# Output projection of a decoder trunk in seven block products, with channels instead of tokens on the partitions

## The chip, the cores and the metric

The kernel runs on one core of a Trainium2 chip. The metric is the time of one execution in device microseconds. The core has a tensor engine (PE, with its weight loads as PEld), a vector engine (DVE), a scalar engine (ACT), GpSimd (POOL) and a queue for transfers (SP). Each works through its own queue in order and waits on semaphores. All data are fp32. A product in full precision is made of three fp32r products of high and low parts: x = xh + xl, w = wh + wl, and x w is taken as xh wh + xl wh + xh wl. The high part is a copy rounded to fp32r, the low part the difference. So each operand of a product costs a copy (ACT) and a subtraction (DVE) before PE can use it, or a copy, an accumulating DMA issued by POOL, and another copy (`split_dma`).

## The reference

Sequence and model width are 1024, the MLP's width is 4096.

```python
        h = rms_norm(x, g_mix[l])
        z = jnp.einsum("bsd,de->bse", h, w_in[l]) + b_in[l]
        ...
        y_a = jnp.einsum("bsc,cd->bsd", u, w_a_out[l])
        ...
        y_b = jnp.einsum("bsc,cd->bsd", v * jax.nn.gelu(gb), w_b_out[l])
        m = jax.nn.sigmoid(sa) * y_a + jax.nn.sigmoid(sb) * y_b
        x = x + jnp.einsum("bsd,de->bse", m, w_o[l])
        h = rms_norm(x, g_mlp[l])
        f = jnp.square(jax.nn.relu(jnp.einsum("bsd,df->bsf", h, w_1[l])))
        x = x + jnp.einsum("bsf,fd->bsd", f, w_2[l])
    return rms_norm(x, g_final)
```

The change lies between `m` and the first products of `w_1`.

## The kernel before

Tokens are split into even and odd ones (two halves of 512), channels into two halves of 512. The products with `w_a_out`, `w_1` and `w_2`, and part of those with `w_in`, are done in a form with seven block products instead of eight: a 2 x 2 block matrix product in which sums and differences of blocks are formed first on either side. A block product here is twelve matmuls (four slices of 128 channels, three products of parts each) of 128 x 128 by 128 x 512, into one PSUM bank. Sums that several outputs share are carried on by copying a bank into another and accumulating further.

The product with `w_a_out` (names beginning with `g_`, lines 1112 to 1239) runs 7 x 4 such blocks: for each of the seven products in the order `GORD`, four pairs of 128-row output tiles. The loop at the end of this part takes a block n a step: it handles what block n-1 left (`g_post`: bank copies on ACT, outputs on DVE), issues block n (`g_mm`), makes the weight parts of block n+4 (`g_lhs`) and the weight sums of block n+5 (`g_sums`), then what the table `GX` lists for this step (`g_parts`: high and low part of a right-hand block; `g_t`: a sum of right-hand blocks; loads). DVE's work goes through `later` and is put out at the step's end by `vector_work`, sorted by the time at which it is expected to be ready. This stage is scheduled by hand (`tc.manual_schedule`): each engine's queue has the order of the text. Its result, multiplied by the gate and added to the other branch, is `m`, channels on partitions.

The output projection with `w_o` is done with tokens on partitions, and in eight blocks: `o_first` takes four token tiles at once through the eight channel slices while `w_o` is loaded and split (`load_wo`), `o_proj` the other four one after the other; 384 matmuls. `residual` adds a row tile of x, takes the sum of squares along the row on ACT, the inverse root (`rms_rows`), scales the row tile, and stores it for the end of the kernel (`x1d`, by a DMA of POOL). Then `transposed` turns the scaled rows by PE into channel tiles, 64 transposes, and `h2_block` evicts them with the gain. The first half's transposes stand between two tiles of the output projection, the second half's after the first two up blocks.

The up products (`up_step`, `up_mm`, `up_lhs`) run for 16 pairs of tiles, seven blocks each; for the first four pairs products 1 and 2 of all come first (they need only the even tokens), then the other five. The down projection follows.

SBUF tiles of 4 KB a partition come from a pool of 37 (`T`) and one of 12 (`M`), half tiles from one of 14 (`EV`); PSUM has eight banks.

## Time and profile before

| | |
|---|---|
| time, median of 3 runs | 1577.55 us (1577.54 to 1577.6) |
| the profiled execution's own time | 1577.67 us |
| its span, first to last instruction | 1575.9 us |
| PE busy | 1552.0 us (98%), 6862 matmuls |
| PEld busy | 1274.2 us (81%) |
| DVE busy | 1179.8 us (75%), 1611 instructions |
| ACT busy | 868.4 us (55%) |
| POOL busy | 156.9 us (10%) |

Busy times are of one profiled execution; matmuls overlap, so PE's busy time is not the time at its peak. The columns of the chain of waits are start, length, engine, tile, line and count; those of the list of waits are the waiting instruction, what it waited for, the total, the count and the longest; those of a timeline are start, length, engine, line, operation, output and input, shape and count, in brackets the idle time before and what ended it; those of a window are its length, then for each engine its busy time and instructions (PE, PEld, DVE, ACT, POOL), the granted clock, the DMA engines' busy share and GB/s. A row of the transfers gives issuing queue, count, size and median time from issue to landing.

### The profile page before, as it was taken

How to read it: one execution, taken by the hardware profiler on the slowest of the kernel's cores; microseconds unless marked ns; L12 is line 12 of the kernel's file. 1: busy time of each engine (PE TensorE's matmuls, PEld its weight loads, DVE VectorE, ACT ScalarE, POOL GpSimd, SP SyncE). 2: the span in 40 equal slices, each digit the busy share in tenths (PEclk: the TensorE clock that was granted, in tenths of full speed). 3: DMA queues.
4: the chain of work that ended last, by engine and by line, in shares of the span. 5: the costliest groups of instructions: out<-in, count | busy, mean ns of one | idle time of the engine just before them, and what ended most of it. 6: DMA issues, size and time to landing. Idle time of an engine off the chain costs nothing.

```text
span 1575.9 us, 19026 instructions
## 1 busy us (share of the span) xinstructions
PE 1552.0 (98%) x6862; PEld 1274.2 (81%) x6862; DVE 1179.8 (75%) x1611; ACT 868.4 (55%) x1183; POOL 156.9 (10%) x190
## 2 busy tenths in 40 slices
PE   8999999999999999999999999999999999999997
PEld 6888778788888888878888877888888888888886
DVE  6799999979899997378667247855554458888897
ACT  5547575667567667345376146554444475555552
POOL 0000000002222222000031000000000001111110
PEclk9999999999999999999999999999999999999999
DMA  9667868899998779944578532533334669888852
GB/s 368 166 158 182 228 178 220 207 266 245 242 249 202 192 187 257 310 148 133 193 184 228 183 112 77 213 113 115 107 108 134 192 215 230 217 223 226 205 121 107
DMA packets 119855, 301.00 MB, mean 191 GB/s; under 512 B 12064, under 2 KB 29984, under 8 KB 119760
## 3 DMA queue, kind: packets, MB, share of 16 engines
q1 hardware_dynamic: 93488, 226.92, 43.9%
q0 software_dynamic: 26128, 72.59, 23.9%
q8 instruction: 54, 0.88, 0.2%
q14 instruction: 41, 0.34, 0.1%
q10 hardware_dynamic: 144, 0.26, 0.1%
HBM read 148.21 MB, written 58.72 MB: 131 GB/s over the span
## 4 chain that ended last, share of the span: by engine, by line
PE 88%; DVE 4%; ACT 3%; issue 2%; DMA 2%; SPq 0%; POOL 0%; ACTq 0%; POOLq 0%; DVEq 0%
PE d L1736 15%; PE z L678 11%; PE yb L1032 8%; PE o L1337 3%; PE e L1851 2%; PE keep L1736 2%; PE o L91 2%; PE z L258 2%; DVE v L438 1%; PE o L1361 1%; PE rg L486 1%; PE rg L488 1%; PE rg L487 1%; DVE y L589 1%; DMA g<-g 1%
## 5 line engine op out<-in xcount | busy, mean ns | idle before, releaser
L678 PE MATMUL z<-xh,win_h 128*128 128x512 f32 x400 | 123.4, 390 | 0.0
L678 PE MATMUL z<-xl,win_h 128*128 128x512 f32 x400 | 123.2, 389 | 0.0
L1748 DVE TENSOR_TENSOR acc<-acc,d 128x1024 f32<-128x1024 f32 x72 | 87.9, 1220 | 33.4 <-PE d L1736 32.7
L678 PE MATMUL z<-xh,win_l 128*128 128x512 f32 x400 | 98.1, 391 | 0.0
L589 DVE SCALAR_TENSOR_TENSOR y<-u,vec,y 128x511 f32<-128x511 f32 (+14 forms) x120 | 88.8, 740 | 0.0
L678 PEld LDWEIGHTS z<-xh,win_l 128*128 128x128 f32 x400 | 75.1, 188 | 16.9
L678 PEld LDWEIGHTS z<-xh,win_h 128*128 128x128 f32 x400 | 75.1, 188 | 16.2
L678 PEld LDWEIGHTS z<-xl,win_h 128*128 128x128 f32 x400 | 75.1, 188 | 15.8
L589 DVE SCALAR_TENSOR_TENSOR yt<-u,vec,yt 128x511 f32<-128x511 f32 (+6 forms) x112 | 82.9, 740 | 0.0
L589 DVE SCALAR_TENSOR_TENSOR y<-yt,csum,y 128x511 f32<-128x511 f32 (+6 forms) x112 | 82.9, 740 | 0.0
L494 ACT ACTIVATE g<-rg,vec 96x1024 f32<-96x1024 f32 x32 | 35.6, 1113 | 84.8 <-PE rg L488 44.5
L1529 ACT ACTIVATE fa<-fa 128x512 f32<-128x512 f32 x16 | 10.1, 632 | 89.8 <-DVE fa L1507 89.8
L438 DVE SCALAR_TENSOR_TENSOR v<-xb,vec,v 128x1023 f32<-128x1023 f32 (+2 forms) x36 | 46.2, 1283 | 16.5 <-ACT v L429 15.7
L1469 ACT ACTIVATE o<-s 128x512 fp32r<-128x512 f32 x64 | 38.2, 624 | 29.4 <-DVE s L1461 26.1
L66 POOL DMA_DIRECT2D win_l<-win_raw x25 | 21.8, 872 | 316.2 <-ACT win_l L65 238.2
L1032 PE MATMUL yb<-hgh,wb_h 128*128 128x512 f32 x168 | 52.5, 394 | 0.0
L1032 PE MATMUL yb<-hgl,wb_h 128*128 128x512 f32 x168 | 51.7, 389 | 0.0
L66 POOL DMA_DIRECT2D zo<-zw x42 | 36.8, 879 | 129.0 <-ACT zo L65 115.8
L998 DVE TENSOR_TENSOR o<-w_raw,o 128x512 fp32r<-128x512 f32 x40 | 27.5, 690 | 29.2 <-ACT o L1469 29.2
L998 DVE TENSOR_TENSOR o<-s,o 128x512 fp32r<-128x512 f32 x64 | 42.6, 687 | 4.7 <-ACT o L1469 4.6
L1372 DVE TENSOR_TENSOR x<-xr,o 128x1024 f32<-128x1024 f32 x8 | 9.7, 1219 | 44.6 <-PE o L1337 30.2
L1032 PE MATMUL yb<-hgh,wb_l 128*128 128x512 f32 x168 | 41.0, 389 | 0.0
(1629 smaller groups left out, 4572.7 us busy)
## 6 DMA issues: line engine op xcount, KB each, us to landing
fr<-fd SPq DMA_DIRECT2D x32, 512.0 KB, 5.9
wr<-in_w_dram SPq DMA_DIRECT2D x32, 512.0 KB, 6.4
w_raw<-in_w_dram SPq DMA_DIRECT2D x31, 512.0 KB, 4.4
zw<-in_w_in_dram SPq DMA_DIRECT2D x28, 512.0 KB, 6.9
win_raw<-in_w_in_dram SPq DMA_DIRECT2D x25, 512.0 KB, 6.8
win_l<-win_raw POOLq DMA_DIRECT2D x25, 512.0 KB, 5.8
zo<-zw POOLq DMA_DIRECT2D x42, 256.0 KB, 5.6
gates<-zg SPq DMA_DIRECT2D x32, 256.0 KB, 4.2
```

Of the source, the lines that this page charges most:

```text
L66: nc.gpsimd.dma_start(l, src, accum_op=ALU.add)
L91: nc.tensor.matmul(ps[:, HALVES[hf]], a, b[hf], start=i == 0, stop=i == len(todo) - 1)
L438: nc.vector.scalar_tensor_tensor(v[:, d:S], a[:, 0:S - d], cbw_c[:, w * 12 + t:w * 12 + t + 1], v[:, d:S], ALU.mult, ALU.add)
L494: nc.scalar.activation(a, gps.pop((n, gi))[:HD, :], AF.Sigmoid, bias=(ba_c, bx_c)[gi][:, n:n + 1])
L589: nc.vector.scalar_tensor_tensor(o[:, k:], a[:, 0:HS - k], c, o[:, k:], ALU.mult, add)
L678: nc.tensor.matmul(zps[s][:, HALVES[hf]], w[:, k, :], xw[k][part][hf], start=n == 0, stop=n == 23)
L998: tt(l, src, h.bitcast(F32), ALU.subtract)
L1032: nc.tensor.matmul(ps[hf], a, b[:, HALVES[hf]], start=n == 0, stop=n == len(todo) - 1)
L1337: nc.tensor.matmul(ps[:, HALVES[hf]], tok(a, k, t), wo[k][b][:, HALVES[hf]], start=k == 0 and b == 0 and n == 0, stop=k == 7 and b == 1)
L1469: nc.scalar.activation(o[:, 0], src, AF.Copy)
L1736: nc.tensor.matmul(o, a, b, start=n == 0 and (p != 1 or g == 0), stop=n == len(todo) - 1, skip_group_check=p == 1 and g > 0)
L1748: tt(acc[p, q2], acc[p, q2], ps, ALU.add)
```

## The change

The output projection becomes a second pass of the seven-product form: all `g_` functions take a letter, "a" for `w_a_out` on the conv branch, "o" for `w_o` on `m`, "u" for the first two products of four pairs of up tiles. One list of 28 + 28 + 8 blocks runs through the same loop. `m` is loaded in the half-token layout (16 transfers of 256 KB instead of 8 of 512 KB), the order of the seven products becomes 1, 2, 6, 7, 4, 5, 3. The output `x1` has channels on partitions; x is loaded transposed (`xt_eo`, a new input) and added to. The rms is taken from channel tiles: ACT squares each output (`x1_squares`), DVE adds the squares of eight tiles, PE sums over partitions with a column of ones (`x1_sums`), a root on 128 x 4 (`x1_root`), and PE spreads its diagonal over the partitions (`x1_spread`); `x1_normed` scales each tile on DVE. The row tiles that the end of the kernel needs are made by 64 transposes of `x1` beside blocks u0 to u5 (`x1_rows`), evicted by ACT and stored by SP. The blocks for products 6, 5, 7, 3, 4 of the first two pairs of up tiles are interleaved; their weight parts, and those of product 2 in the new loop, are made by `split_dma` instead of DVE. `o_first`, `o_proj`, `residual`, `rms_rows`, `transposed`, `h2_block`, `h2_sum`, `h2_parts` and `first_lhs` go away. PSUM banks stay one pool to the end of the up products.

The core of the diff:

```diff
-    GORD = (1, 2, 6, 5, 3, 7, 4)
+    GORD = (1, 2, 6, 7, 4, 5, 3)
...
+    gseq = [(w, i, p) for w in "ao" for p in GORD for i in range(GP)]
+    gseq += [("u", i, p) for p in (1, 2) for i in range(AHEAD)]
...
+        if p in (1, 7) or w != "u" and p == 2:
             nc.scalar.activation(o[:, 0], src, AF.Copy)
             later(at("A", 0.6), 0.63, low, o[:, 1], src, o[:, 0])
         else:
             split_dma(src, o[:, 0], o[:, 1])
...
         else:
+            d = x1[i // 2, o, i % 2][:, HALVES[m_]]
+            later(0, 0.63, tt, d, d, src, ALU.add)
+            squares.append((o, d))
...
     def g_post(w, i, p):
...
+            gb[*k, "f"], gb[*k, "u"] = bank(f"g{w}{i}f"), EV(f"gu{w}{i}")
+            nc.scalar.activation(gb[*k, "f"], gb[*k, "b"], AF.Copy)
+            nc.scalar.activation(gb[*k, "u"], gb[*k, "b"], AF.Copy)
             at("A", 1.24)
+        elif p == 7:
+            gb[*k, "c"] = EV(f"gc{w}{i}")
+            nc.scalar.activation(gb[*k, "c"], gb[*k, "f"], AF.Copy)
+            at("A", 0.62)
+        elif p == 4:
+            g_out(w, i, 1, 0, gb[*k, "f"])
+        else:
+            c = gb[*k, "c" if p == 5 else "u"]
+            later(0, 0.63, tt, c, c, gb[*k, "e"], ALU.add)
+            g_out(w, i, int(p == 5), 1, c)
...
+    def x1_squares():
+        while squares:
+            o, d = squares.pop(0)
+            tile_ = EV if o == 0 else lambda n: T(n)[:, 0:HS]
+            sqn[0] += 1
+            a = tile_(f"xs{o}_{sqn[0]}")
+            nc.scalar.activation(a, d, AF.Square)
+            ready = at("A", 0.62)
+            if o not in ss:
+                ss[o] = a
+            else:
+                later(ready, 0.63, tt, ss[o], ss[o], a, ALU.add)
+    def x1_sums(o):
+        rbk[o] = bank(f"ss{o}")
+        for i in range(4):
+            nc.tensor.matmul(rbk[o][:, i:i + 1], ss[o][:, i * P:(i + 1) * P], ones[:, 0:1],
+                             start=True, stop=True)
+        at("P", 0.5)
+    def x1_root(o):
+        st = cp.tile([P, 4, 4], F32, tag="st4", name=f"stm{o}", bufs=2)
+        v, s, t, r = (st[:, i, :] for i in range(4))
+        nc.vector.tensor_scalar(v, rbk[o][:, 0:4], 1.0 / D, EPS, ALU.mult, ALU.add)
+        newton_rstd(r, v, s, t)
+        at("V", 1.5)
+        ss[o] = rd = EV(f"rdm{o}") if o == 0 else T(f"rdm{o}")[:, 0:HS]
+        for i in range(4):
+            d = rd[:, i * P:(i + 1) * P]
+            if i % 2 == 0:
+                nc.vector.tensor_scalar(d, ident, r[:, i:i + 1], None, ALU.mult)
+            else:
+                nc.scalar.activation(d, ident, AF.Copy, scale=r[:, i:i + 1])
+        at("V", 0.4)
+    def x1_spread(o):
+        rbk[o] = bank(f"rbm{o}")
+        for i in range(4):
+            d = slice(i * P, (i + 1) * P)
+            nc.tensor.matmul(rbk[o][:, d], ones, ss[o][:, d], start=True, stop=True)
...
+    def x1_normed(kk, o):
+        for c2 in range(2):
+            src = x1[kk, o, c2]
+            hq[kk, o, c2] = a = src if o else T(f"hq{kk}{o}{c2}")
+            for i in range(2):
+                c = 4 * kk + 2 * c2 + i
+                dve(0.68, 0, nc.vector.scalar_tensor_tensor, a[:, HALVES[i]], src[:, HALVES[i]],
+                    gmlp_c[:, c:c + 1], rbk[o], ALU.mult, ALU.mult)
+    def x1_rows(t):
+        rows, c0 = T(f"x1r{t}"), t % 4 * P
+        for kk in range(2):
+            ps = bank(f"tr{t}{kk}")
+            for c in range(4):
+                nc.tensor.transpose(ps[:, c * P:(c + 1) * P],
+                                    x1[kk, t // 4, c // 2][:, c % 2 * HS + c0:c % 2 * HS + c0 + P],
+                                    ident)
+            nc.scalar.activation(rows[:, HALVES[kk]], ps, AF.Copy)
+            at("A", 0.62)
+        nc.sync.dma_start(x1d[t], rows)
...
     def up_lhs(i, p):
...
+        if i < 2:
+            split_dma(src, o[:, 0], o[:, 1])
+        else:
+            nc.scalar.activation(o[:, 0], src, AF.Copy)
+            low(o[:, 1], src, o[:, 0])
...
+          13: ((m_load, 0, 1),), 14: ((g_parts, "a", 5, 0), (m_load, 1, 1)),
+          15: ((g_parts, "a", 5, 1),), 18: ((g_parts, "a", 3, 0), (g_load, "o", 0, 0)),
+          19: ((g_parts, "a", 3, 1), (g_load, "o", 1, 0)), 20: ((g_load, "o", 2, 0),),
+          21: ((g_load, "o", 3, 0), (g_parts, "o", 1, 0)), 22: ((g_parts, "o", 1, 1),),
+          23: ((g_load, "o", 0, 1),), 24: ((g_parts, "o", 2, 0), (g_load, "o", 1, 1)),
+          25: ((g_parts, "o", 2, 1), (g_load, "o", 2, 1)), 26: ((g_load, "o", 3, 1),)}
+    o0 = GP * 7
+    GX.update({o0 + n: v for n, v in {
+        1: ((g_t, "o", 0, 1),), 2: ((g_t, "o", 0, 2), (g_t, "o", 1, 1), (x_in, 0, 0)),
+        3: ((g_t, "o", 1, 2), (x_in, 1, 0)), 4: ((g_parts, "o", 6, 0),), 5: ((g_parts, "o", 6, 1), (g_t, "o", 0, 3)),
+        6: ((g_t, "o", 1, 3),), 8: ((g_parts, "o", 7, 0), (g_t, "o", 0, 4)),
+        9: ((g_parts, "o", 7, 1), (g_t, "o", 1, 4)), 12: ((g_parts, "o", 4, 0),),
+        13: ((g_parts, "o", 4, 1), (x_in, 0, 1)), 14: ((x_in, 1, 1),), 16: ((g_parts, "o", 5, 0),),
+        17: ((g_parts, "o", 5, 1), (up_load, 0, (0,))), 18: ((up_load, 1, (0,)),),
+        19: ((g_parts, "o", 3, 0), (up_load, 2, (0,))), 20: ((g_parts, "o", 3, 1), (up_load, 3, (0,))), 22: ((x1_sums, 0),), 23: ((x1_root, 0),),
+        24: ((x1_spread, 0),), 25: ((x1_normed, 0, 0),), 26: ((g_parts, "u", 1, 0), (g_parts, "u", 1, 1),
+                                                             (x1_normed, 1, 0)),
+        27: ((g_parts, "u", 2, 0), (g_parts, "u", 2, 1))}.items()})
+    u0 = 2 * o0
+    GX.update({u0 + n: v for n, v in {
+        0: ((x1_rows, 4), (x1_sums, 1), (x1_rows, 5), (x1_root, 1)),
+        1: ((x1_rows, 6), (x1_rows, 7), (x1_spread, 1), (x1_normed, 0, 1)),
+        2: ((x1_rows, 0), (x1_normed, 1, 1), (g_t, "u", 0, 1), (g_t, "u", 1, 1)),
+        3: ((x1_rows, 1), (g_t, "u", 0, 2), (g_t, "u", 1, 2), (up_load, 0, (1,))),
+        4: ((x1_rows, 2), (g_parts, "u", 6, 0), (up_load, 1, (1,))), 5: ((x1_rows, 3), (g_parts, "u", 6, 1)),
+        6: ((g_parts, "u", 5, 0), (up_lhs, 0, 6)), 7: ((g_parts, "u", 5, 1), (up_lhs, 1, 6))}.items()})
...
+            x1_squares()
             g_get(n - 1, g_post)
+            if n == u0:
+                vector_work(clk["V"])
+                to_mlp()
...
+    useq = [(i, p) for p in ORDER[1:4] + (3, 4) for i in range(2)]
+    useq += [(i, p) for i in range(2, AHEAD) for p in ORDER[1:4] + (3, 4)]
+    useq += [(i, p) for i in range(AHEAD, NP) for p in ORDER]
+    UX = {0: ((g_t, "u", 0, 3), (g_t, "u", 1, 3)), 1: ((g_parts, "u", 7, 0), (g_parts, "u", 7, 1)),
+          2: ((g_t, "u", 0, 4), (g_t, "u", 1, 4)), 3: ((g_parts, "u", 3, 0), (g_parts, "u", 3, 1)),
+          5: ((g_parts, "u", 4, 0), (g_parts, "u", 4, 1))}
```

525 lines of the change are left out of this document (184 added, 341 removed).

## The prediction

> **What bounds the kernel now.** I read the page first, then the chain of work that ended last, the tensor engine's waits, and the vector engine's timeline.
>
> ```profile
> span 1575.9 us, 19026 instructions
> PE 1552.0 (98%) x6862; PEld 1274.2 (81%) x6862; DVE 1179.8 (75%) x1611; ACT 868.4 (55%) x1183; POOL 156.9 (10%) x190
> 774.17 2.72 PE g0a L1171 x12
> ...
> 850.96 43.52 PE o L1337 x192
> 894.48 22.03 PE o L91 x96
> ...
> 943.75 3.01 PE f0a L1478 x12
> 949.49 3.49 PE tr_m L1407 x32
> ...
> 1256.09 5.44 PE keep L1736 x24
> ```
>
> TensorE (PE) is the bound: 98% busy, and the chain lies on it. 192 products take 43.52 us, 0.2267 us each; I call twelve of them (2.72) a block. A transpose costs 3.49/32 = 0.109. The change works between 774.17, where the product with w_a_out starts, and 1256.09, where the down projection starts. From 850.96 PE has 384 products of the output projection (`o`), 1344 up products and 64 transposes: 87.0 + 304.6 + 7.0 = 398.7 us, in 405.1. So 6.5 us are lost there, 4.1 of it in these waits (without g3e's, which lies before 850.96) and the rest in slow restarts and late operands (f0a's twelve take 3.01 instead of 2.72: 0.3 for a restart):
>
> ```profile
> PE f0a L1478 <- DVE x L1372: 1.4, 1, 1.4
> PE f0c L1478 <- DVE fa L1505: 1.0, 1, 1.0
> PE f0c L1478 <- DMA b3l<-hq: 0.8, 1, 0.8
> PE f0d L1478 <- DVE fa L1507: 0.6, 1, 0.6
> PE g3e L1171 <- DMA ga<-gs: 0.3, 1, 0.3
> PE o L91 <- ACT hq L1401: 0.3, 1, 0.3
> ```
>
> **What PE gains.** The seven-product form needs 4 x 7 blocks = 336 products instead of 384. The 64 transposes stay (now they make the residual's rows). Added are 16 small products for the sums of squares (two instructions for each fp32 product) and 16 for spreading the root:
>
> ```profile
> 6.86 0.56 PE L312 MATMUL spare<-stx,ones 128*128 128x1 f32 x2 [6.86 <-ACT x L201]
> 7.28 5.04 PE L316 MATMUL spare<-ident,ones 128*128 128x128 f32 x22
> 14.31 1.50 PE L316 MATMUL spare<-ident,ones 128*128 128x128 f32 x12
> 32.33 1.06 PE L224 MATMUL rb<-rd,ones 128*128 128x128 f32 x8
> ```
>
> Eight of L224's take 0.9 from start to start, so 1.8 for the spread of both halves. The sums' products have one column instead of 128; the only such row is L312's (two in 0.56, with PE just woken), so a half's eight cost between 0.9 and 2.2; I take 0.9, since here PE comes straight from other products: 1.8 again. Without any wait the end of the up products is at 774.17 + 672 x 0.2267 (152.3) + 304.6 + 7.0 + 3.6 = 1241.7: 14.4 us earlier. The question is how much of it VectorE (DVE) and the transfers take back.
>
> **What DVE must do for it.** Its real price is the distance from start to start:
>
> ```profile
> 781.87 0.69 DVE L414 TENSOR_TENSOR gs<-wa,wa 128x512 f32<-128x512 f32 x1
> 782.60 0.69 DVE L414 TENSOR_TENSOR gs<-gs,wa 128x512 f32<-128x512 f32 x1
> 783.33 0.69 DVE L414 TENSOR_TENSOR wa<-wa,gs 128x512 f32<-128x512 f32 x1
> 783.94 0.68 DVE L414 TENSOR_TENSOR wa<-wa 128x512 f32<-128x512 f32 x1
> 784.54 1.22 DVE L414 TENSOR_TENSOR q<-q,q 128x1024 f32<-128x1024 f32 x1
> 785.67 0.69 DVE L998 TENSOR_TENSOR ga<-wa,ga 128x512 fp32r<-128x512 f32 x1
> 35.48 0.74 DVE L228 SCALAR_TENSOR_TENSOR xc<-xc,vec,rb 128x512 f32<-128x512 f32 x1
> 36.14 0.69 DVE L233 TENSOR_TENSOR xl<-xc,xh 128x512 fp32r<-128x512 f32 x1
> ```
>
> 512 columns: 0.61, or 0.72 when the next needs its result; 1024 columns: 1.13; scaling by the root: 0.66. The rows above stand in the order of the text, each as soon as the one before lets it, so the queue can be walked by adding. I number blocks a0-a27 (w_a_out), o0-o27, u0-u7 (first up products), and add up the queue block by block against 2.72.
>
> First pile, a21 to o9. From a21 to a27 the outputs, the high/low parts of m and of w_o come to 21.3 in 19.0: 2.3 behind at o0. o0 to o9 come to 2.7, 1.7, 2.9, 4.4, 3.8, 5.5, 4.4, 1.2, 4.1, 3.5 = 34.2: o3, for one, has a pair's four weight sums (2.7), one sum of m (1.1) and a low part (0.6); o5 an output (0.6), four weight sums, a sum of m and product 6's second low part (1.1 each). So the last of them, the low part of product 7's second half, is done 36.5 after the start of o0. o12 starts at 12 x 2.72 = 32.6 and needs it with its eighth product, at about 34.3: PE waits 2.2. (With 2 us more or less in the pile it would be 0 to 4.) After that DVE has slack to o20.
>
> Second pile, counted from the start of o20. PE does o20-o22 and the sums of squares (8.2 + 0.9 = 9.1). The root (`x1_root`) stands in DVE's queue ahead of the outputs of o22 and all that follows, so DVE, done with o21's outputs at 6.8, idles until then, and everything behind waits with it. What the root costs:
>
> ```profile
> 28.14 0.17 DVE L208 TENSOR_SCALAR stx<-stx 128x4 f32<-128x4 f32 x1 [1.39 <-ACT x L201]
> ...
> 29.59 0.48 DVE L215 TENSOR_SCALAR rd<-ident,stx 128x128 f32<-128x128 f32 x2
> 710.68 1.28 ACT L96 ACT_TABLE_LOAD   x1 [6.75 <-DVE lv L1095]
> ```
>
> 1.9 from 28.14 to 30.07, and 1.3 for the table of the square root, which started only when its operand was there: DVE is free at 12.4. The outputs of products 5 and 3 then cost 1.33 a block, squares 0.61, the low part of an up weight 0.61; beside them stand eight scalings (5.3) and four low parts (4.5) of the normed block. Queue: outputs and squares of o22 (1.9) and o23 with a low part (2.6) to 16.9, at o25 four scalings and the like to 22.1 (5.2), o26 to 27.3 before its two low parts, which end at 28.4 and 29.5, o27 to 34.3, last output 35.7, last sum of squares 36.9. PE, after o24, the spread and three blocks, wants the first low part at 23.7: it waits 4.7. u0 ends at 28.4 + 11 x 0.2267 = 30.9. Next in PE's queue stand eight transposes of a row tile of the second half, the last four of which need the output done at 35.7, and the second half's sums of squares, due 31.8, started 36.9: 5.1 more, and u1 stands behind it. From there PE's own work (sums, 8 x 8 transposes, spread, u1-u7) covers the second half's root and scalings, and ends 63.9.
>
> Up weights of the first two pairs go through GpSimd's (POOL's) accumulating DMA instead of DVE:
>
> ```profile
> ga<-gs POOLq DMA_DIRECT2D x8, 256.0 KB, 3.3
> ga<-wa POOLq DMA_DIRECT2D x8, 256.0 KB, 7.2
> 785.59 0.62 ACT L65 ACTIVATE ga<-gs 128x512 fp32r<-128x512 f32 x1
> 786.11 0.63 ACT L67 ACTIVATE ga<-gs 128x512 fp32r<-128x512 f32 x1
> 788.78 1.05 ACT L1123 ACTIVATE g5h<-q 128x1024 fp32r<-128x1024 f32 x1
> 812.00:832.00 20.00, 19.68 (x88) 15.94 (x87) 12.62 (x17) 13.43 (x23) 5.26 (x6) 1.00 1.05 266
> 774.00:851.00 77.00, 76.68 (x338) 63.17 (x337) 59.43 (x81) 48.38 (x79) 16.63 (x19) 1.00 0.84 220
> ```
>
> Block (0,6)'s sums stand behind product 6's second low part, whose high part ScalarE (ACT) makes only after it has evicted the last row tile (59): high part 60, low 61.1, sums 62.5, copy 63.1, landing 3.3 later 66.4; PE wants it at 64.3. With the next block 2.6 in all. 3.3 is the row of the same kind of source; with 7.2 it would be 6.5.
>
> Free by their cover: ACT (48.4 of 77 us busy in the first product, the fourth pair of the window's row) takes the 16 squares, 0.52 each. x comes in as 8 x 512 KB as before, only transposed. The rows' store moves from POOL to SP's queue, ahead of two loads of up weights; the second row tile's is issued at 51.9 (u3 and its transposes end 51.4, eviction 0.5), so the load lands about 58, 2 us before its sums: no wait, but no more cover than that. POOL loses the row stores and gains the splits of the up weights; it is 10% busy.
>
> **Sum.** -14.4; +0.6 (lost in the first product before, too: 76.8 for 76.2), +2.2, +4.7, +5.1, +2.6, +1.2 (four restarts of 0.3): **+2.0 us**.
>
> One more price. After its longest wait PE ran at half rate (the rows at 6.86, 7.28 and 14.31 above): 22 products in 5.04, later 12 in 1.5: about 4.8 us at half rate, 2.4 lost. After the 1.4 of f0a there was none of that. My two waits, 4.7 and 4.3 (the 5.1 is cut by eight transposes), lie between 1.4 and 6.9, a little nearer 6.9: each costs 0 to 2.4, and I take one of them at 2.4. [...] Forecast: **+4.4**. The profiled execution took 1577.67 by its time (span 1575.9), 0.12 above the median 1577.55; so 1582.1, against the median **1582.0 us**.
>
> **Rivals.**
> The same walk with PE at full rate after the waits: +2.0, 1579.6 us. For it: the waits are short of 6.9, and neither is wholly empty. Within 0.2% (3.2 us, about what a measurement of this kernel can tell from no change). Chance 0.34.
>
> Faster: the second pile doesn't form, because the low parts of u0 and the last outputs get through DVE before 23.7 and 31.8, that is 4.7 and 5.1 us sooner; the compiled queue would have to put them before the scalings, or the root would have to be ready before PE's sums. Then +0.6, +2.2, +2.6 and 0.9 stay: -8.1, 1569.4 us. For it: in the first product DVE is busy 59.4 of 77 us; against it: the rows of DVE above come one by one in the order of the text. It decides by the sum of the two waits: 9.8 us in the walk; the sign turns where it is 7.8, and below 4.6 the kernel is faster by over 0.2%. Chance 0.19.
>
> Slower still: the loads of w_o (8 x 512 KB) start at a18, when the transfers were already full. From 812 to 832 the DMA share was 1.05 at 266 GB/s. Some 2 MB more by a22 are 7.5 us; the low parts for products 5 and 3 go out four blocks (10.9) ahead and take 7.2, so 3.8 of it would reach PE: 1585.8. g3e's 0.3 is the one such wait so far. Chance 0.13.
>
> That the products aren't fewer has no chance worth a number: the loops give 28 blocks.
>
> **How the numbers follow.** Forecast (half rate once or twice) 0.34, the late loads 0.13: slower 0.47. Full rate: same 0.34. No second pile: faster 0.19. The range leaves out half of the fast case and the sum of both slow ones with two cold restarts: 1570 to 1588. The likeliest case alone: 1580.8 to 1586 (one or two half-rate spells, 7.2 instead of 3.3 for a landing).
>
> **What would show it.** Right: 28 `g_mm` blocks for `o`, 76 us long; the up products' end 1258 to 1261; a wait of 4 to 5 us of the first up block for DVE's low part, another for the last residual sums before the second sums of squares, 2 us of p7's first block, 2 to 3 us of up block (0,6) for a POOL DMA; products 0.43 apart for some us after the long waits. Wrong: DVE idle between o24 and u0 (no pile), PE waiting for loads in the first product, or the two long waits under 4.6 us in all, which would make it faster.

## The result, and the profile after

| | before | after |
|---|---|---|
| time, median | 1577.57 us (1577.54 to 1578.67, 4 runs) | 1601.47 us (1599.63 to 1604.37, 4 runs) |
| profiled execution: time, span | 1577.67, 1575.9 us | 1604.37, 1602.6 us |
| from the first `w_a_out` product to the first down product | 774.01 to 1255.92: 481.9 us | 775.80 to 1282.28: 506.5 us |

The ratio is 1.0151 (95% interval 1.0134 to 1.0169): 23.9 us slower. The forecast was 1582.0, range 1570 to 1588: the direction was right, the time lies outside. Of the 26.7 us between the two profiled executions 24.6 lie in the section of the last row; 1.8 come before it, where the change does nothing (in the profiles below this start lies anywhere from 772.6 to 775.8), 0.3 after it. So I compare kernels below by their times and, where a few us matter, by the length of this section.

The first lines of the page of after; PE does 16 matmuls fewer (48 fewer products, 32 small ones more) and is busy for longer:

```profile
span 1602.6 us, 19168 instructions
PE 1559.4 (97%) x6846; PEld 1278.1 (80%) x6846; DVE 1225.3 (76%) x1647; ACT 895.0 (56%) x1235; POOL 169.6 (11%) x202
```

PE's waits in the section, after (waiting instruction, what it waited for, total us, count, longest). A name is that of the PSUM bank that PE writes: go0f is a bank of the first pair in the output projection, gu0a the bank of block u0, f2c a bank of the third pair of up tiles; tr are the transposes, ss the sums of squares:

```profile
PE f2c L1389 <- DVE fa L1415: 5.6, 1, 5.6
PE gu0a L1179 <- DVE gu1l L989: 3.8, 1, 3.8
PE f1d L1389 <- DMA o<-w_raw: 3.0, 1, 3.0
PE f4a L1389 <- ACT u L1407: 2.7, 1, 2.7
PE f0b L1389 <- DMA o<-s: 2.5, 1, 2.5
PE go0f L1179 <- DVE go7l L989: 1.8, 1, 1.8
PE tr L1311 <- DVE x L405: 1.1, 1, 1.1
PE ss L1267 <- DVE xs L405: 1.0, 1, 1.0
PE f0d L1389 <- DVE gu4l L989: 0.4, 1, 0.4
```

Five of these the forecast had (go0f, gu0a, tr, ss, f0b). Four it had not, and they come later: f0d, f1d, f2c and f4a, in the up products (f4a belongs to the fifth pair). By stages, the windows of after (length, then busy time and instructions of PE, PEld, DVE, ACT, POOL, then granted clock, DMA share, GB/s):

```profile
934.30:977.73 43.43, 37.51 (x178) 30.91 (x176) 28.91 (x43) 24.79 (x45) 3.61 (x5) 0.84 0.46 145
977.73:1004.00 26.27, 23.79 (x97) 19.18 (x97) 17.75 (x21) 18.58 (x29) 8.56 (x10) 0.94 0.60 112
1004.00:1067.00 63.00, 51.30 (x204) 40.80 (x203) 37.19 (x58) 27.65 (x40) 0.00 (x0) 0.92 0.42 146
1067.00:1282.28 215.28, 215.28 (x951) 178.17 (x951) 115.31 (x176) 99.48 (x146) 1.74 (x2) 1.00 0.38 128
```

From 1004 to 1067 PE stands still for 11.7 us at a granted clock of 0.92. The same stretch of before had 280 matmuls, no idle time and 1.00:

```profile
1004.00:1067.00 63.00, 63.00 (x280) 52.18 (x279) 41.11 (x67) 30.99 (x48) 0.00 (x0) 1.00 0.33 117
```

In the whole section PE waits 21.9 us, against 4.4 before. Beside that, products lie 0.43 us apart instead of 0.227 behind most of these waits. By starts that loses 1.6 us behind go0f, 2.4 and 2.1 behind u0 and the sums, 1.5 behind f0b, 2.7 behind f2c and 1.4 behind f4a: 11.7.

Two other rows show what the up section waits for. SP's queue, after, around the loads for the third pair:

```profile
972.98 0.32 SPq L1316 DMA_DIRECT2D x1d<-x1r  x1
1001.44 0.32 SPq L1441 DMA_DIRECT2D fd<-fa  x1
1001.87 1.71 SPq L1348 DMA_DIRECT2D w_raw<-in_w_dram  x3
```

For 28 us SP issues nothing: a store of the first pair's result (`fd<-fa`) heads its queue and waits for its data, and the loads of the next weights stand behind it. When they go, they meet the last `split_dma` of the second pair, issued at 1002.23. Its row among the transfers of after (issuing queue, count, size, us to landing; 3.3 in the forecast):

```profile
o<-w_raw POOLq DMA_DIRECT2D x1, 256.0 KB, 8.7
```

That is f1d's wait. And DVE's queue starts on the third pair only when the first load lands:

```profile
1008.48 0.69 DVE L1364 TENSOR_TENSOR s<-w_raw 128x512 f32<-128x512 f32 x1 [2.08 <-DMA w_raw<-in_w_dram]
```

### The profile page after: what moved, and what is told of

Read it like the earlier page. It is cut to its first block, busy times and chain, and to the rows that moved or that the text cites. A ratio compares the mean times of both kernels' runs of the same rounds, so it can differ in the third digit from the quotient of the medians.

```text
span 1602.6 us, 19168 instructions
## 1 busy us (share of the span) xinstructions
PE 1559.4 (97%) x6846; PEld 1278.1 (80%) x6846; DVE 1225.3 (76%) x1647; ACT 895.0 (56%) x1235; POOL 169.6 (11%) x202
## 5 line engine op out<-in xcount | busy, mean ns | idle before, releaser
L989 DVE TENSOR_TENSOR o<-s,o 128x512 fp32r<-128x512 f32 x56 | 38.5, 690 | 43.3 <-ACT o L1380 43.3
L1380 ACT ACTIVATE o<-s 128x512 fp32r<-128x512 f32 x56 | 34.5, 624 | 54.9 <-DVE s L1365 37.8
L66 POOL DMA_DIRECT2D db_1l<-wr x7 | 6.1, 870 | 320.4 <-ACT db_1l L65 297.3
L65 ACT ACTIVATE zo<-zw 128x512 fp32r<-128x512 f32 x42 | 26.3, 625 | 20.7 <-PE z2f L840 2.1
```

The source lines that it names most:

```text
L65: nc.scalar.activation(l, src, AF.Copy, scale=-1.0)
L66: nc.gpsimd.dma_start(l, src, accum_op=ALU.add)
L989: tt(l, src, h.bitcast(F32), ALU.subtract)
L1380: nc.scalar.activation(o[:, 0], src, AF.Copy)
```

## Experiments

The question was where the 20 us between forecast and result came from: from the half-rate spells (12 in the trace, 2.4 in the forecast), from the second pile, or from the late waits. Each ratio is to the kernel before, with its 95% interval.

| kernel | time | ratio | section |
|---|---|---|---|
| after | 1601.5 | 1.0151 (1.0134 to 1.0169) | 506.5 |
| e1_fill | 1601.1 | 1.0136 (1.0119 to 1.0152) | 503.6 |
| e2_stores | 1593.8 | 1.0099 (1.0084 to 1.0114) | 498.2 |
| e3_sums | 1603.4 | 1.0161 (1.0146 to 1.0176) | 508.5 |
| e4_high_first | 1600.9 | 1.0143 (1.0128 to 1.0158) | 504.3 |
| e5_parts | 1593.8 | 1.0101 (1.0086 to 1.0116) | 497.3 |
| e6_order | 1599.9 | 1.0138 (1.0123 to 1.0153) | 503.8 |
| e7_ring | 1583.7 | 1.0041 (1.0024 to 1.0057) | 490.3 |
| e8_all | 1576.5 | 1.0000 (0.9991 to 1.0010) | 481.6 |
| e9_late | 1590.7 | 1.0087 (1.0072 to 1.0102) | 495.6 |
| e10_fill8 | 1576.7 | 0.9993 (0.9984 to 1.0003) | 482.2 |
| e11_u0 | 1575.7 | 0.9989 (0.9980 to 0.9998) | 479.7 |
| e12_loads | 1573.3 | 0.9976 (0.9966 to 0.9985) | 478.3 |
| e13_fill7 | 1585.6 | 1.0047 (1.0033 to 1.0060) | 488.2 |
| e14_shift | 1575.4 | 0.9986 (0.9976 to 0.9995) | 479.0 |

A second table was the key to most readings. It gives, for five places and the end, the moment at which PE could go on (or went on without a wait), in us from the start of the section, taken from PE's timeline of each profiled execution ("product 3" and "product 2" are those of the seven):

| | u0's 2nd product | second sums of squares | f0b | f2c, product 3 | f4a, product 2 | down projection |
|---|---|---|---|---|---|---|
| after | 162.7 | 171.4 | 205.1 | 251.5 | 287.1 | 506.5 |
| e1_fill | 162.6 | 171.3 | 205.0 | 251.4 | 284.5 | 503.6 |
| e2_stores | 162.6 | 171.3 | 203.4 | 247.9 | 279.3 | 498.2 |
| e5_parts | 160.9 | 167.3 | 197.7 | 244.1 | 277.8 | 497.3 |
| e7_ring | 162.6 | 171.3 | 205.1 | 242.8 | 272.7 | 490.3 |
| e8_all | 160.9 | 167.1 | 195.4 | 232.2 | 262.2 | 481.6 |

One thing in it no edit made. u0's first product starts at 158.4 to 158.5 in after, e1, e2, e7 and e10, and at 156.8 to 156.9 in e5, e8, e9 and e13, though their edits touch nothing before the last blocks of the output projection: go0f waits 1.8 us in all of them, but in the last four no half rate follows (the last section says more). These 1.6 us stand in all later columns of e5 and e8. Likewise e2's f0b is 1.7 earlier than after's, ahead of anything that its edit touches: a spell of half rate behind the second sums was shorter in that execution (7.9 us from there to the spread of the second root, 9.5 in after).

**The waits filled (e1).**

```diff
+        if (w, i, p) == ("u", 0, 1):
+            spare(gb[w, i, b], 14)
...
+    def spare(ps, count):
+        a = gh["u", 1, 0]
+        for _ in range(count):
+            nc.tensor.matmul(ps, a[:, 0:P], a[:, 0:HS], start=True, stop=True)
...
+    SPARE = {(0, 6): (0, "b", 10), (1, 4): (2, "b", 12), (2, 3): (3, "b", 22), (4, 2): (5, "a", 10)}
```

> The kernel after, with 68 extra products of 512 columns whose sums are thrown away, put on TensorE right ahead of five of its waits: 14 before the first up product (wait 3.8 us), 10 before f0b (2.5), 12 before f1d's product 4 (3.0), 22 before f2c's product 3 (5.6), 10 before f4a's product 2 (2.7). They change no operand and no order on another engine; at 0.227 each they fill most of each wait and lengthen none. Theory A (the products at 0.43 us behind the waits come from TensorE having stood idle): the waits for operands stay, filled, but the half-rate spells behind u0, f0b, f2c and f4a go (2.4 + 2.1 + some 3 in the transposes and sums between + 1.5 + 2.7 + 1.4 = about 13 us lost in the trace of after, less what DVE then makes TensorE wait in the transposes): 8 to 12 us less than after, 1590 to 1594. Theory B (the slow spells come from something else that happens at these places, such as transfers or operand reads): the spells stay, and the time is that of after, 1601, or a little more.

Half of theory A holds. The spells behind u0, f0b, f2c and f4a are gone from the trace (8.0 of the 11.7 us), so they do come from PE standing still; those behind go0f and the second sums stay. But 8 to 12 us were expected and little came: 1601.1, with the interval of the ratio reaching from no gain to some 5 us, and 2.9 in the section, all of it behind f2c. The table tells why. The sums of squares, f0b's weights and f2c's bank came free at the same moments to 0.2 us, although PE was earlier at each. What it gained up to there it waited away, as in this row of PE's waits in e1 (1.1 in after):

```profile
PE tr L1318 <- DVE x L405: 3.8, 1, 3.8
```

So most of the half rate that was removed lay under the work of other engines. The spell that stayed, behind the second sums, is another matter (e5).

**The stores out of SP's queue (e2).**

```diff
-        nc.sync.dma_start(fd[i, :, 0:2, :], a...)
+        (nc.gpsimd if i < 4 else nc.sync).dma_start(fd[i, :, 0:2, :], a...)
...
-            nc.sync.dma_start(fd[i, :, 2:4, :], fb[i]...)
+            (nc.gpsimd if i < 4 else nc.sync).dma_start(fd[i, :, 2:4, :], fb[i]...)
```

> The kernel after, with the eight stores of the up products' results of the first four pairs issued on GpSimd's queue instead of SyncE's; nothing else. In the trace of after the loads of the third pair's up weights are issued at 1001.87, right behind the first such store, which waits 28.1 us for its data, and the fifth pair's last loads at 1054.03 behind another one. Theory A (those loads stand in the queue behind the stores, and from that come f2c's wait of 5.6 us and f4a's of 2.7): the loads go out some us earlier, f2c's wait falls below 2 us and f4a's to 0, and with the half-rate spells behind them (2.7 and 1.4) the time is 8 to 11 us less, 1590 to 1593; f1d's 3.0 goes too if its weight transfer no longer competes with the same loads. Theory B (the loads wait for free tiles, or the wait is made by VectorE and ScalarE passing work to and fro): waits as before within 1 us, time 1600 to 1603.

1593.8, 7.7 less. The loads for the third pair go out at 988.76 instead of 1001.87; f1d's and f4a's waits are gone. But f2c's is not: 6.4 us. The rows ahead of it, DVE's timeline in e2 and then ACT's:

```profile
1009.13 0.68 DVE L1424 TENSOR_TENSOR fb<-f0d,u 128x512 f32<-128x512 f32 x1
1012.55 0.69 DVE L989 TENSOR_TENSOR o<-s,o 128x512 fp32r<-128x512 f32 x1 [2.74 <-ACT o L1380]
1013.16 0.68 DVE L1424 TENSOR_TENSOR fb<-f1d,u 128x512 f32<-128x512 f32 x1
1016.58 0.69 DVE L989 TENSOR_TENSOR o<-w_raw,o 128x512 fp32r<-128x512 f32 x1 [2.73 <-ACT o L1380]
```

```profile
1009.85 1.06 ACT L1425 ACTIVATE fb<-fb 128x1024 f32<-128x1024 f32 x1 [1.36 <-DVE fb L1424]
1010.94 1.06 ACT L1426 ACTIVATE fb<-fb 128x1024 f32<-128x1024 f32 x1
1011.91 0.61 ACT L1380 ACTIVATE o<-s 128x512 fp32r<-128x512 f32 x1
1013.88 1.06 ACT L1425 ACTIVATE fb<-fb 128x1024 f32<-128x1024 f32 x1 [1.36 <-DVE fb L1424]
```

Read them by time, from one fence to the other. DVE adds (1009.13), ACT takes Relu and square of that (1009.85, 1010.94), then copies a weight (1011.91), DVE takes that copy's low part (1012.55), then the next add, and so on. Each idle time in brackets is the other engine's turn. A turn takes 4.0 us and feeds one block, which PE does in 2.72. In a turn DVE works for 1.4 us and ACT for 2.7, so neither looks full by its busy share.

**Turn-taking broken (e7, with the stores moved; e9, without).**

```diff
+            for f, *a in held_posts[:]:
+                f(*a)
+            held_posts.clear()
             up_step(*useq[n])
...
-            nc.scalar.activation(fb[i], fb[i], AF.Relu)
-            nc.scalar.activation(fb[i], fb[i], AF.Square)
+            if i < AHEAD:
+                held_posts.append((up_last, i))
...
+        if i < AHEAD and (i, "q") not in done:
+            done.add((i, "q"))
+            held_posts.append((up_first, i))
+            return
```

> The run with the stores on GpSimd's queue, and in it the Relu and the square of the up outputs of the first four pairs issued on ScalarE one block later, behind the next block's copy of weights. In that run f2c still waited 6.4 us: VectorE's queue before it alternates with ScalarE's, add (0.7), Relu and square (2.1), copy (0.6), low part (0.7), some 4.0 us a block where TensorE needs 2.7. Theory A (that turn-taking makes f2c's wait): the copy no longer waits for the add, the turn is 2.7 or less, f2c's wait falls below 2 us, and the time is 4 to 7 us less than with the stores moved alone: 1587 to 1590. Theory B (the look-ahead of four blocks, or the buffers for the weights' parts, makes the wait): f2c waits 5 us or more, 1592 to 1595.

1583.7, 10 less than with the stores alone: theory A, and 3 us better than its range. (The profiled execution took 1587.3, the longest of its four, so e7's section is long for its time.) No wait after f0d is left in the up products; PE's waits in the section in e7:

```profile
PE gu0a L1179 <- DVE gu1l L989: 3.8, 1, 3.8
PE f0b L1389 <- DMA o<-s: 2.5, 1, 2.5
PE go0f L1179 <- DVE go7l L989: 1.8, 1, 1.8
PE tr L1311 <- DVE x L405: 1.2, 1, 1.2
PE ss L1267 <- DVE xs L405: 1.0, 1, 1.0
PE f0d L1389 <- DMA o<-w_raw: 0.7, 1, 0.7
```

These are the waits of the forecast and 0.7 more.

> The kernel after, with Relu and square of the up outputs of the first four pairs issued on ScalarE one block later, and the stores left on SyncE's queue; nothing else. With the stores moved as well the same edit was worth 10 us. Theory A (ScalarE and VectorE take turns, which alone makes most of f2c's wait; the loads behind the stores are a second, separate delay): f2c's wait is shorter by 3 us or more, but the loads go out later, since the stores they stand behind now wait one block longer: 1592 to 1597, a gain smaller than 10. Theory B (the later Relu and square holds the loads back by as much as it gives): no gain, 1600 to 1604.

1590.7: 10.8 less than after, more than I expected, and in another place. f2c waits 4.8 (DVE stands 5.0 us for the late load), but f1d and f4a do not wait at all. The second pair's last weight copy had also stood behind Relu and square: ACT now takes it at 992.1 instead of 1001.3, so its transfer goes out before the loads do. After, stores, later Relu and square, both: 1601.5, 1593.8, 1590.7, 1583.7. The two gains add up (7.7 + 10.8 = 18.5, both together 17.8; by the intervals each is known to some 3 to 4 us).

**DVE's second pile (e3, e5).**

```diff
-                later(ready, 0.63, tt, ss[o], ss[o], a, ALU.add)
+                nc.gpsimd.tensor_tensor(ss[o], ss[o], a, ALU.add)
```

> The kernel after, with the fourteen additions that sum the squares done by GpSimd instead of VectorE; nothing else. Theory A (VectorE's queue is the pile that makes u0 wait 3.8 us and the transposes and second sums of squares 2.1): four of the additions stand between the root and u0's low part, six behind the root in all, 0.6 us each, so u0 waits 1.4 instead of 3.8, the transposes and sums nothing or little; with a shorter half-rate spell 5 to 10 us less, 1591 to 1596. Theory B (GpSimd takes so long for an addition, or slows VectorE so much while both work, that the sums of squares come later than now): the wait before the sums of squares grows, of both halves, and the time is 1602 or more.

1603.4: theory B, though 1.9 us more than after is within the error. The additions left DVE's queue, and its queue was no shorter: u0 waits 2.5 instead of 3.8, but only because PE reaches it 2.0 later, and the second sums start 3.0 later (174.4). The same two low parts in DVE's timeline, first in after, then in e3, and the GpSimd addition that ran beside them and one that ran alone:

```profile
942.00 2.36 DVE L989 TENSOR_TENSOR gu2l<-hq,gu2h 128x1024 fp32r<-128x1024 f32 x2
```

```profile
942.00 3.42 DVE L989 TENSOR_TENSOR gu2l<-hq,gu2h 128x1024 fp32r<-128x1024 f32 x2
```

```profile
942.34 2.00 POOL L1262 TENSOR_TENSOR xs<-xs,xs 128x512 f32<-128x512 f32 x1 [3.27 <-ACT xs L1257]
947.60 1.26 POOL L1262 TENSOR_TENSOR xs<-xs,xs 128x512 f32<-128x512 f32 x1 [3.27 <-ACT xs L1257]
```

Beside one GpSimd addition the two low parts took 1.06 us longer (3.42 for 2.36), more than the 0.61 that the addition saved DVE; the addition beside them took 2.00 us, the one alone 1.26. How the two hold each other up these runs do not show.

```diff
+        if w == "u" and p in (1, 2):
+            split_dma(src, h, l)
+            at("A", 2.0)
+            return
...
-        if p in (1, 7) or w != "u" and p == 2:
+        if w != "u" and p in (1, 2, 7):
```

> The kernel after, with the low parts of the normed operand of products 1 and 2 (four of 1024 columns) and of the up weights of product 1 (four of 512) made by ScalarE copies and GpSimd's accumulating DMA instead of VectorE; nothing else. That takes 4 x 1.18 + 4 x 0.61 = 7.2 us out of VectorE's queue between the root and the last square. The chain from the second sums of squares on (root, spread, scalings, products 6's parts, weight sums) is in the trace of after a row of VectorE and ScalarE work. Theory A (VectorE's pile sets when the second sums of squares start, and with it all that follows): the sums start some 5 to 7 us earlier against the end of the o blocks, f0b, f1d, f2c and f4a each start so much earlier, and the time is 4 to 6 us less, 1595 to 1597, though u0 still waits for its low part (landing after 3.3 to 7 us instead of VectorE's 3.8 wait). Theory B (the up section sets its own pace by the loads behind the stores and by ScalarE and VectorE working by turns): the gain is lost again in f1d's, f2c's and f4a's waits, less than 2 us, 1599 to 1602.

1593.8, 7.7 less, somewhat more than theory A. The sums of squares start 4.1 us earlier, and f0b and f2c each come free 7.4 earlier, f4a 9.3: the pile lies on a chain that reaches through the up section, though its own wait at u0 has not become shorter (3.7).

The 7.4 have three parts. 1.6 are there before u0 and not the edit's (see below the table). 2.5 come from there to the second sums. The other 3.3 come between the second sums and the spread, where PE does the same 8 sums, 24 transposes and block u1 without a wait in both kernels. PE's rows for this stretch, after, e5, and e1 (length, busy time and matmuls, granted clock, DMA share, GB/s; a count takes in neighbours that overlap the edges):

```profile
947.18:956.73 9.55, 9.54 (x45) 0.64 0.57 160
```

```profile
940.63:946.84 6.21, 6.21 (x47) 1.00 1.04 270
```

```profile
946.47:955.97 9.50, 9.50 (x45) 0.64 0.52 152
```

In after the transposes and sums had waited 2.1 just before, in e5 not at all. From the spread to f0b it is 24.2 in both, as in e2, e3, e7 and e9 to 0.1. So this spell of half rate does lie on the path and costs 3.3 us, and the filling of e1 had not removed it.

**Products in another order (e4), steps moved (e6), all together (e8).**

```diff
+        if (w, i, p) in (("o", 0, 7), ("u", 0, 1)):
+            prods = prods[0::3] + prods[2::3] + prods[1::3]
...
+        if i < 2:
+            prods = prods[0::3] + prods[1::3] + prods[2::3]
```

> The kernel after, with the twelve products of some blocks in another order: the four of high part by high part first, then the others, those with the operand that comes last at the end (block o product 7 of pair 0, block u0, and the up blocks of the first two pairs). A low part that came too late for the 2nd or 3rd product of a block is then needed at its 9th. Theory A (waits are set by when the low part is ready, so each is shorter by the products put ahead of it): o product 7 waits 1.8 - 0.7 = 1.1, u0 3.8 - 1.6 = 2.2, f0b 2.5 - 1.4 = 1.1, f1d 3.0 - 1.4 = 1.6; u0's 1.6 comes back as a wait of the transposes, since VectorE's queue ends when it did. 3.5 us less waiting, and 3 less of half rate where a wait falls to 1.1: 1594 to 1597. Theory B (the half rate is set by the whole of the waits and not by their length): only the 3.5 us, 1598.

1600.9, within the error of after. Most waits shrank as expected (go0f 0.9, f0b 1.1, f1d 1.7, gu0a 2.6 in two), and others grew by nearly as much: the transposes 4.3, f2c 6.9. Both theories expected too much, as in e1: shorter waits of PE give little while the releasing engine is no earlier.

```diff
-        0: ((x1_rows, 4), (x1_sums, 1), (x1_rows, 5), (x1_root, 1)),
-        1: ((x1_rows, 6), (x1_rows, 7), (x1_spread, 1), (x1_normed, 0, 1)),
+        0: ((x1_rows, 4), (x1_sums, 1), (x1_root, 1), (x1_rows, 5)),
+        1: ((x1_spread, 1), (x1_rows, 6), (x1_rows, 7), (x1_normed, 0, 1)),
...
-        4: ((x1_rows, 2), (g_parts, "u", 6, 0), (up_load, 1, (1,))), 5: ((x1_rows, 3), (g_parts, "u", 6, 1)),
+        4: ((g_parts, "u", 6, 0), (x1_rows, 2), (up_load, 1, (1,))), 5: ((g_parts, "u", 6, 1), (x1_rows, 3)),
```

> The kernel after, with three steps moved in the queues: the second root ahead of the row tile that ScalarE evicts before it (its square root started 2.1 us after its operand), the spread of the second root ahead of sixteen transposes (1.75 us of TensorE), and product 6's high parts ahead of two row tiles' evictions (1.5 and some 2.5 us on ScalarE). Theory A (the chain from the second sums of squares to f0b is a chain through TensorE, ScalarE and VectorE, and each of these steps lies on it): f0b's wait of 2.5 us and its half-rate spell go, and the chain that follows on VectorE and ScalarE moves forward by the same 3 to 5 us: 1596 to 1599. Theory B (as in the run before, the up section's own pace decides): under 2 us, 1599 to 1602.

1599.9. f0b's wait fell to 0.6, the section by 2.7 us, the time by 1.5, which the intervals do not separate from nothing: nearer theory B.

> The three edits before in one kernel, with the stores on GpSimd's queue: parts by DMA, the three steps moved, Relu and square one block later. If the second pile, the chain to f0b and the turn-taking are separate and follow each other, the gains add: 7.7 for the stores, 4 to 7 for the turns, 4 to 6 for the parts, 3 to 5 for the order: 1575 to 1583, near the kernel before. If they cover each other, it is no better than the best of them, 1587 to 1590.

1576.5: e2, e5, e6 and e7 together reach the time before. The gains nearly add: 7.7 (stores), 10.1 (later Relu and square), 7.7 (parts) and 1.5 (steps) are 27.0, together 25.0.

**The price of half rate, again (e10, e13).** The same 14 spare products ahead of u0, in e8 and, with ten ahead of f0b, in e7.

> The kernel of all three edits and moved stores, with 14 spare products of 512 columns ahead of the first up product, where TensorE still waits 3.7 us for u1's low part and then loses 2.8 at half rate. The same filling of five waits in the kernel after changed its time by only 0.4 us. Theory A (there the lost half rate lay under other engines' work, here TensorE is the bound behind u0): 2 to 3 us less, 1573.5 to 1574.5. Theory B (the half-rate spell is covered here too): within 0.7 us of 1576.5.

Nearer theory B: 1576.7, by the ratios 1.1 less than e8, which the intervals do not separate from nothing. In the trace the spell behind u0 is gone (2.8), but u0 now waits twice, 0.5 and 1.3, the second time for the second half of its low part. (The section is 0.5 longer than e8's because go0f's wait has a spell behind it here, 1.6; without that it would be some 1 us shorter.)

> The kernel with stores moved and Relu and square one block later, with spare products whose sums are thrown away: 14 ahead of u0 (wait 3.8) and 10 ahead of f0b (2.5). In that kernel no wait follows f0b but 0.7, and 2.4 + 2.1 + 1.5 us are lost at half rate behind the two waits, and some more in the transposes between. Theory A (half rate costs time where no later wait takes it up): f0b's 1.5 go, u0's partly, since the transposes wait for VectorE's last residual sum either way: 1.5 to 4 us less than 1583.7, 1579.7 to 1582.2. Theory B (covered here too): within 0.7 us of 1583.7, and the waits for operands grow by what the half rate no longer takes.

Theory B again: 1585.6, not less than 1583.7. In the trace the section is 2.1 shorter, but 1.6 of that are there before u0, so 0.5 are left for the filling; the transposes wait 3.8 instead of 1.2, and from the second sums to the spread PE still needs 9.4 us (e7: 9.5).

**Towards a better kernel (e11, e12, e14).** e11 changes e8 at both piles; this is part of its diff to e8.

```diff
-        if w == "u" and p in (1, 2):
+        if w == "u" and p == 2:
             split_dma(src, h, l)
...
-        24: ((x1_spread, 0),), 25: ((x1_normed, 0, 0),), 26: ((g_parts, "u", 1, 0), (g_parts, "u", 1, 1),
-                                                             (x1_normed, 1, 0)),
-        27: ((g_parts, "u", 2, 0), (g_parts, "u", 2, 1))}.items()})
+        24: ((x1_spread, 0),), 25: ((x1_normed, 0, 0), (g_parts, "u", 1, 0), (g_parts, "u", 1, 1)),
+        27: ((x1_normed, 1, 0),)}.items()})
```

> The kernel of all three edits and moved stores, with u0's low parts back on VectorE but right behind the four scalings that they need, ahead of the four scalings of product 2; product 2's parts go behind the second root; the weights' low parts of o product 2 go by DMA too (four of 0.61 less in the first pile), and o product 7 of pair 0 and u0 take the low part of their operand in their last four products. Theory A: no wait at u0 (3.7 and 2.8 of half rate gone), o product 7's 1.8 gone; but the second sums of squares start no earlier than VectorE's queue lets them (2.3 us more in it), so 2 to 4 us of it come back as a wait of the transposes or of f0b: 4 to 6 less, 1570.5 to 1572.5. Theory B (VectorE and ScalarE set the whole stretch from the root to f0b): all of it comes back there, 1575 to 1577.

1575.7: the waits at u0 and go0f are gone (in e8 3.7, 1.8, and 2.8 of half rate), and all but 1 to 2 came back at the transposes, the sums and f0b, and as half rate: from the second sums to the spread PE needs 7.0 us in e11 at a granted clock of 0.64, and 4.5 in e8 at 1.00, for the same instructions. Theory B, nearly.

```diff
+        0: ((up_load, 0, (1,)), (up_load, 1, (1,)), (x1_rows, 4), (x1_sums, 1), (x1_root, 1), (x1_rows, 5)),
...
+        4: ((up_lhs, 0, 6), (g_parts, "u", 6, 0), (x1_rows, 2)), 5: ((g_parts, "u", 6, 1), (x1_rows, 3)),
+        6: ((up_lhs, 1, 6), (g_parts, "u", 5, 0)), 7: ((g_parts, "u", 5, 1),)}.items()})
```

> The kernel of the run before, with the loads of the second halves of the first two pairs' up weights issued ahead of the row tiles' stores on SyncE's queue, and the weight sums and copies of blocks (0,6) and (1,6) ahead of product 6's and product 5's high parts. If f0b is held by its weights (it waited for a POOL transfer in every run so far), what comes back at f0b in the run before goes: 1 to 3 us less than it, 1568 to 1571. If it is held by product 6's low parts instead, or the early loads wait for free tiles and hold up the stores behind them, the same or up to 2 us more.

1573.3, 2.4 less than e11, as expected of the difference: f0b no longer waits. (The loads and the order of the sums were moved in one run and are not told apart.) At 0.9976 of the time before this kernel beats both. What is left of PE's waits in it, the larger ones:

```profile
PE tr L1318 <- issue: 1.6, 1, 1.6
PE tr L1318 <- DVE x L405: 1.5, 1, 1.5
PE ss L1274 <- DVE xs L405: 1.0, 1, 1.0
PE f1c L1396 <- DMA o<-s: 0.9, 1, 0.9
```

Beside them stands the half rate: the stretch from the second sums to the spread takes 7.8 us at a granted clock of 0.56, 3.3 more than in e8.

> The best kernel so far, with block u1 ahead of the second half's transposes and sums of squares on TensorE (the row tiles, the root, the spread and what follows one block later). There the transposes and sums waited 4.1 us for VectorE's last residual sums and squares, and 1.8 were lost at half rate behind them. Theory A (these waits lie on the path): u1 fills 2.7 of them: 2 to 4 less, 1569 to 1571. Theory B (the chain from the second sums through root, scalings and product 6 to f0b is the path, and one block less now covers it): the wait moves to f0b, within 1 us of 1573.3.

1575.4: theory B, and a little worse. The first two of these waits shrank, and f1b (0.8), f0c (1.9) and the spread (1.8) wait instead.

## Why the prediction was wrong

It was right in direction, and right in most of its steps. The section was to lose 18.8 us to waits and the like against a floor of 467.5 (506.5 - 39.0); it lost 39.0. Term by term, from the trace of after:

| term | forecast | measured |
|---|---|---|
| o12 (go0f), first pile | 2.2 | 1.8 |
| u0, second pile | 4.7 | 3.8 |
| transposes and second sums | 5.1 | 2.1 |
| up blocks (0,6), (1,6) | 2.6 | 2.5 |
| restarts and the rest, transposes at half rate included | 1.8 | 5.4 |
| half rate between products | 2.4 | 11.7 |
| f0d, f1d, f2c, f4a | none | 11.7 |

The walk through DVE's queue held: both piles formed where it put them, and three of the four waits came within 0.9 us. The fourth, the transposes and second sums, was 2.1 for 5.1 because PE came to it late, at half rate: with u0's wait filled (e1) it was 3.8 + 1.0. The step that failed is the end of that walk: "From there PE's own work (sums, 8 x 8 transposes, spread, u1-u7) covers the second half's root and scalings", and after product 6's blocks the sum went back to PE alone. The walk should have gone on, with ACT and SP in it, to the fourth pair of up tiles. The changed list lets the first two pairs run interleaved, so their Relus, squares and stores come together, ahead of the next pair's copies (ACT) and loads (SP). The text counted ACT as free by its busy share, and of SP's queue it looked at two loads among the row stores, none later. The runs show what that cost: without the two delays the same change takes 1583.7 (e7), 1.7 above the forecast and inside its range.

The half rate was mis-sized as a term, 11.7 for 2.4, but most of it is not where the time went. Where it was removed by filling, it gave 2.9 us of the section in after (8.0 of the 11.7 removed), 0.5 in e7 and some 1 in e8, and in no case a time that its error separates from no change. One spell did cost its length: that behind the second sums, 3.3 us with its transposes, which e5 removed and no filling did. The forecast added one spell to the waits as if PE alone set what follows; it depends on whether PE is then what the next engine waits for, as from the sums to the spread, or waits itself. Its rule that a wait counts by its length was wrong too (below). The rival with the late loads of `w_o` had the right kind of cause and the wrong loads: PE had no wait for a transfer of `w_o`. The rival on the faster side needed the second pile not to form; it formed.

How the 24 us divide is shown only as far as the runs divide them: 17.8 are removed with the stores and the later Relu and square, 7.7 with the second pile's low parts (the half rate behind the second sums included), and e8 with both and the moved steps takes 25 off. That the interleaving of the two pairs is what brought Relus, squares and stores together was read from the queues and not run by itself.

## To carry to other kernels

When a change puts work earlier on one engine, walk every queue on from there until PE meets operands that the change does not touch: the dear waits here lay 75 to 130 us behind the last product of the output projection, on queues with idle time in them. Two engines that hand each other work by turns, and a store that waits at the head of the queue of loads, show as idle brackets naming each other, not as busy shares. Before pricing a wait of PE or a slow spell, look whether the next release moves with it: compare the moments of release between two kernels, and what does not move is not yours to win. In these runs a slow spell cost its length where PE worked through to what another engine waited for (3.3 us behind the second sums), and little where PE itself waited at the end of it (2.9 us for the 8.0 filled in e1).

## What the hardware showed unexpectedly

The half rate did not follow the length of the wait before it. Cut in after where the granted clock changes, PE's rows (length, busy time and matmuls, granted clock, DMA share, GB/s):

```profile
889.68:893.09 3.41, 3.41 (x9) 0.50 0.92 289
893.09:937.46 44.37, 41.60 (x191) 1.00 0.56 115
937.46:944.29 6.83, 5.81 (x16) 0.50 0.00 0
944.29:947.70 3.41, 1.28 (x10) 1.00 0.00 0
947.70:954.53 6.83, 6.83 (x24) 0.50 0.61 192
954.53:981.84 27.31, 24.82 (x137) 1.00 0.64 193
981.84:985.25 3.41, 3.41 (x10) 0.50 0.94 159
985.25:1026.21 40.96, 33.09 (x144) 1.00 0.62 173
1026.21:1033.04 6.83, 5.69 (x14) 0.50 0.21 80
1033.04:1063.76 30.72, 28.03 (x124) 1.00 0.34 120
1063.76:1067.17 3.41, 3.41 (x10) 0.50 0.00 0
```

Half rate lasted 3.41 or 6.83 us, three times each, and the stretches at full rate between were 1, 8, 9, 12 and 13 times 3.41 us long, to 0.04 us. Cut finer, into windows of 3.41 us whose edges lie within 0.06 us of these:

```profile
978.38:981.79 3.41, 0.93 (x5) 1.00 0.45 77
981.79:985.20 3.41, 3.41 (x10) 0.51 0.93 157
985.20:988.61 3.41, 3.41 (x17) 0.99 0.88 151
```

```profile
1005.68:1009.09 3.41, 2.30 (x11) 1.54 (x9) 1.33 (x3) 1.69 (x2) 0.00 (x0) 1.00 0.93 284
1009.09:1012.50 3.41, 1.52 (x7) 1.26 (x8) 3.32 (x7) 1.15 (x2) 0.00 (x0) 1.00 1.04 341
1012.50:1015.91 3.41, 3.41 (x17) 2.83 (x16) 2.53 (x5) 0.73 (x2) 0.00 (x0) 1.00 0.97 387
```

The first three rows: f0b's wait of 2.5 us falls into one window, and the whole next window runs at 0.51. The other three, with all engines' columns: f1d's wait of 3.0 is cut by a boundary, and no slow window follows. Between 700 and 1300 us of after, the windows at full rate with up to 1.16 us idle were followed by full rate, six with 1.82 to 3.41 by half rate, and the second of these three, with 1.89, by full rate (in before, behind f0a's wait of 1.4, the granted clock stayed at 1.00). Of the windows at half rate in after, the two with 1.01 and 1.14 us idle were followed by half rate again; of the seven with none, six were followed by full rate and one, from 947.70 on, by half rate, in the stretch of transposes and one-column products behind the second sums. So idle time is not the whole of it, and what else counts is not shown. Nor does the length of a wait say it: go0f's wait of 1.8 cost 1.6 us in after and nothing in e5, and f1d's of 3.0 cost nothing.

In after, the nine `split_dma` of 256 KB for up weights issued between 977 and 997 landed after 3.3 to 4.4 us, and the one issued beside the loads of 512 KB after 8.7.
